# A hybrid attention encoder block on one Trainium2 core: v of the neighbourhood heads kept by head, column and row, and gate products handed out differently

## Chip, core and metric

The kernel runs on one core of one Trainium2 chip. The metric is the device time of one execution in microseconds (us); lower is better. All inputs and weights lie in the chip's memory (DRAM) when it starts, and the output goes back there. The instruction streams are those of TensorE (PE, with its weight loads listed apart as PEld), VectorE (DVE), ScalarE (ACT), GpSimd (POOL), and SyncE (SP), which does nothing but issue transfers.

## What is computed

One encoder layer over 1024 tokens of width 1024, in float32. The parts that matter here:

```python
a = rms_norm(x, g_mix)
qa, ka, va, qd, kd, vd, gate_na, gate_dil = split(a @ w_in)
# mixer A: 8 heads of 64 on a grid of 16 rows x 64 columns; each query sees a
# clamped window of 8 rows x 16 columns, with a learned bias per head
y_na  = neighborhood_attention(heads(qa, 8), heads(ka, 8), heads(va, 8), rpb)
# mixer B: 3 groups of 4 heads, banded attention at dilation 1, 4, 16 (rotary q, k)
y_dil = dilated_attention(rotary(heads(qd, 12)), rotary(heads(kd, 12)), heads(vd, 12))
h = x + (sigmoid(gate_na) * (y_na @ W_A) + sigmoid(gate_dil) * (y_dil @ W_B)) @ w_out
h = h + relu(rms_norm(h) @ w_up) ** 2 @ w_down
h = h + sigmoid(rms_norm(h) @ w_ple_gate) * (p @ w_ple_proj)
out = rms_norm(h)
```

In mixer A a score is q.k/8 plus the bias, and positions outside the window get -1e30 through the bias; then comes a softmax and the product with v.

## The kernel before

Every float32 matrix product is done on rounded operands: an operand is split into a high part (a copy or cast on ACT, line 107 of the helper `split`) and a low part (a subtraction on DVE or POOL, line 108), and three products hi.hi, hi.lo, lo.hi are summed (`mm3`, lines 206 to 208). Buffers come from tile pools of fixed size; a tile that is asked for again waits until the readers of its last use are done. The program is written once, and a scheduler with a model of the engines then decides the order in which each engine gets its instructions; where the code says `keep_in_program_order`, as for all PE work of the attention, that order is the written one. Each engine works through its own list in order, so an instruction that waits holds up all behind it on that engine. SP's list of transfers is such a list too.

The stages, in order of time: the normalised input and the v columns of `w_in` (`v_unit`, five units of 256 columns; u = 0 and 1 are the neighbourhood heads), written to `v_scr` in DRAM as [token][head][128], where the 128 are the high and low halves of 64; then q and k by ten fast-product units (`unit`, their results in `ps_q`), written to `qk_scr`; then attention; then the branch products with `W_A` and `W_B` (`ps_b`), and the rest of the layer, which the change does not touch.

**Attention** is a list of tiles: 96 dilated ones (3 groups of 32) and then 64 neighbourhood ones (8 heads x 4 column blocks `cb` x 2 query halves `qt`). One step of the loop takes three tiles at different stages (`AHEAD` = 3): the tile three steps on gets its scores (PE into `sc`, lines 629 and 630; then DVE adds bias or mask and takes the extreme of the row, line 637; then ACT takes the exponential, line 639), and the present tile is turned (PE transposes into `tp_p`, line 717 for the neighbourhood and 846 to 852 for the dilated groups; ACT and DVE split it into `pt_h` and `pt_l`) and multiplied with v (`av`). In the neighbourhood, DVE takes the reciprocal `rs` of the sum (line 707) and POOL scales the tile by it (line 708) before it is turned. DVE forms the smallest of (score with its sign turned + bias with its sign turned), so that the result can be handed to the exponential as it is. For that, POOL turns the sign of each loaded bias tile in place (line 692).

`na_loads` brings the data of the next column block: a bias tile, and v as four transfers of 64 KB each, one for each group `gq` of four grid rows (line 678).

The **gate products** (`gates()`, into `ps_g`, line 594) depend on nothing in the attention and fill PE there. They come in 256 steps of three products of 512 columns; each 16 steps need one weight unit, loaded into `w_raw` (line 137) and split into `w_hi` and `w_lo` (lines 154, 155). `FILL_HEAD` steps stand ahead of the first tile, `FILL_DIL` are paid for each dilated tile, `FILL_NA` for each neighbourhood tile; what is left comes behind the last tile.

Of the kernel before, what the change touches and what calls it, by code (L numbers as in the profile page):

```python
# [9 lines left out]
F32 = mybir.dt.float32  # L10
F32R = mybir.dt.float32r
I32 = mybir.dt.int32
AF = mybir.ActivationFunctionType
ALU = mybir.AluOpType
# [3 lines left out]
P = 128  # L18
# [6 lines left out]
GW = 64  # L25
NEG = -1e30
EPS = 1e-6

FILL_HEAD = 24
FILL_DIL = 1.5  # L30
FILL_NA = 1.35

AHEAD = 3

# [5 lines left out]
KC0 = (0, 8, 24, 32)  # L40
# [19 lines left out]
def encoder_kernel(ctx: ExitStack, tc: tile.TileContext, t: dict, out: bass.AP):  # L60
    nc = tc.nc
# [23 lines left out]

    p_scr = scr.tile([S, D], F32, name="p_scr")
    v_scr = scr.tile([S, 20 * P], F32, name="v_scr")
    g_scr = scr.tile([16, P, S], F32, name="g_scr")

    qk_scr = scr.tile([20, 2, 2, 64, S], F32, name="qk_scr")  # L90
# [13 lines left out]
    def split(hi, lo, src, scale=None, lo_eng=None):  # L104
        eng = nc.vector if lo_eng is None else lo_eng
        if scale is None:
            nc.scalar.copy(hi, src)  # L107
            eng.tensor_tensor(lo, src, hi.bitcast(F32), op=ALU.subtract)  # L108
        else:
            nc.scalar.activation(hi, src, AF.Copy, scale=scale)  # L110
            eng.scalar_tensor_tensor(lo, src, scale, hi.bitcast(F32), op0=ALU.mult, op1=ALU.subtract)
# [183 lines left out]
    with ExitStack() as st:  # L295
# [83 lines left out]
        def v_unit(u):  # L379
            w2 = take(2, 2)  # L380
            for tp_ in range(4):
                ps = ps_mm.tile([P, HALF], F32, name="ps_v", tag="mm")
                pv3 = ps.rearrange("p (a b) -> p a b", a=2)
                for a in range(2):
                    mm_tok(pv3[:, a, :], w2, tp_ * 2 + a)
                stg = qp.tile([P, 2, 4, P], F32R, name="v_stage", tag="nat")
                s4 = ps.rearrange("p (a h d) -> p a h d", a=2, h=4)
                split(stg[:, :, :, 0:64], stg[:, :, :, 64:128], s4)
                dst = v_scr[tp_ * 256:(tp_ + 1) * 256, u * HALF:(u + 1) * HALF]
                dma(dst.rearrange("(a p) c -> p a c", p=P), stg.rearrange("p a h d -> p a (h d)"))  # L390

# [182 lines left out]
    with ExitStack() as st:  # L574
# [48 lines left out]
        def score(sc, qs, ks, kl, qsl, ksel, n):  # L623
# [5 lines left out]
            pe(nc.tensor.matmul(o, qs[:, qsl], kk, start=True, stop=False))  # L629
            pe(nc.tensor.matmul(o, qs[:, qsl], ll, start=False, stop=True))  # L630

        def soft(sc, bias, n, m_out=None, s_out=None):
            s_ = aa.tile([P, 384], F32, name="s_sb", tag="s_sb", bufs=4)
            nm = m_out if m_out is not None else ap.tile([P, 1], F32, name="nm", tag="nm", bufs=4)
            sm = s_out if s_out is not None else ap.tile([P, 1], F32, name="sm", tag="sm", bufs=4)

            nc.vector.tensor_tensor_reduce(s_[:, :n], sc[:, :n], bias, 1.0, 3.0e38,  # L637
                                           op0=ALU.add, op1=ALU.min, accum_out=nm)
            nc.scalar.activation(s_[:, :n], s_[:, :n], AF.Exp, bias=nm, scale=-1.0, accum_out=sm)  # L639
            return s_, sm  # L640
# [24 lines left out]
        def na_loads(h, cb):  # L665

            if h > 7:
                return
            if cb % 2 == 0:
                na_vt[h, cb // 2] = aa.tile([P, 2, 4, P], F32R, name="v_t", tag="v_t", bufs=3)  # L670
            if cb == 2:
                na_bt[h, 2] = na_bt[h, 1]
            else:
                na_bt[h, cb] = ap.tile([P, 2, 384], F32, name="bias", tag="bias", bufs=3)
                nc.sync.dma_start(na_bt[h, cb], t["na_bias"][h // 2, CT[cb], :, h % 2])
            for gq in range(4):
                src = v_scr.rearrange("(g r c) f -> g c r f", c=GW, r=4)[gq, KC0[cb]:KC0[cb] + 32, :, h * P:(h + 1) * P]
                nc.sync.dma_start(na_vt[h, cb // 2][:, cb % 2, gq, :].bitcast(F32), src)

        def na_score(h, cb, qt, env):  # L680
            j, e = h // 2, h % 2
            if cb == 0 and qt == 0:
                env_head[h] = ready_ops.pop(0)
            if cb == 1 and qt == 0 and h < 7:
                load_raw(h + 1)
            if cb == 2 and qt == 1 and h < 7:
                ready_ops.append(operands(h + 1))
            if qt == 0:
                na_loads(*((h, cb + 1) if cb < 3 else (h + 1, 0)))
                if cb != 2:  # L690
                    bt = na_bt[h, cb]
                    nc.gpsimd.tensor_scalar(bt, bt, -1.0, 1.0, op0=ALU.mult, op1=ALU.mult)
            env["vt"] = na_vt[h, cb // 2]
            qs, ks, kl = env_head[h]
            sc = ps_sc.tile([P, HALF], F32, name="sc", tag="sc")
            o = qt * HALF + cb * P

            def ksel(a):
                return a.rearrange("p (g x) -> p g x", g=4)[:, qt:qt + 3, 4 * KC0[cb]:4 * KC0[cb] + P]

            score(sc, qs, ks, kl, slice(o, o + P), ksel, 384)
            env["pr", cb, qt] = soft(sc, na_bt[h, cb][:, qt, :], 384)

        def na_norm(cb, qt, env):
            pr, sm = env["pr", cb, qt]
# [266 lines left out]
        def pay(upto):  # L972
            while debt[0] >= upto:
                debt[0] -= 1.0
                next(fill, None)

        load_raw(8)
        load_piece(10)
        for b in range(2):
            dma(flat2(act[1][0][b]), a_scr[b])  # L980
        load_raw(9)
# [553 lines left out]
```

## Time and profile before

| what | value |
|---|---|
| time, median of 3 runs | 1693.76 us (1688.40 to 1694.41) |
| the profiled execution: its own time | 1693.16 us |
| the profiled execution: span from first to last instruction | 1691.3 us |
| mean granted TensorE clock | 0.969 of full speed |
| busy: PE, DVE, ACT, POOL | 1566.1, 1191.8, 707.4, 677.9 us |
| moved by transfers | 279.22 MB, 165 GB/s on average |

The busy times are unions over the span: 93% for PE means that PE had a product under way in 93% of the time, not that each ran at full clock. A share of the whole span is a mean over stages with different limits, so the rows further on are cut by stage.

### The profile page before, as it was taken

The numbers are of one execution on the slowest core, as the hardware profiler recorded it, in microseconds if no ns is written. First come the engines' busy times: TensorE is split into PE (matmuls) and PEld (weight loads), VectorE is DVE, ScalarE is ACT, GpSimd is POOL, SyncE is SP. The second block draws the span as 40 slices with busy tenths as digits, with TensorE's granted clock in tenths as the row PEclk, the third lists the DMA queues.
The fourth block names the chain that finished last, engine by engine and source line by source line (L and its number), as shares of the span: only waits on it lengthen the run. The fifth ranks groups of instructions, "written<-read, shape, count | busy, mean of one in ns | idle before, by whom it ended". The sixth has DMA issues, their size and how long they took to land. (4 is left out here: it accounts for less than half of the span.)

```text
span 1691.3 us, 22551 instructions
## 1 busy us (share of the span) xinstructions
PE 1566.1 (93%) x7787; PEld 1308.3 (77%) x7787; DVE 1191.8 (70%) x2016; ACT 707.4 (42%) x1325; POOL 677.9 (40%) x459
## 2 busy tenths in 40 slices
PE   8899999959999988869998799999998999999998
PEld 7899777747788777747787588888876788887886
DVE  6844799622565677755556977667777999999955
ACT  7322222214777766664333433333345333332422
POOL 0332678512333233333402777777743332225100
PEclk9999999988999999989999799999999999999999
DMA  8443455672576678774533244444457545433122
GB/s 310 173 150 108 142 150 161 199 267 89 171 220 186 205 232 253 208 231 156 174 137 131 92 139 147 157 164 143 137 191 279 177 162 163 149 112 118 51 97 71
DMA packets 122353, 279.22 MB, mean 165 GB/s; under 512 B 15392, under 2 KB 39936, under 8 KB 121728
## 3 DMA queue, kind: packets, MB, share of 16 engines
q1 hardware_dynamic: 116480, 267.29, 48.2%
q10 hardware_dynamic: 5760, 10.49, 1.7%
q8 instruction: 62, 1.02, 0.3%
q14 instruction: 51, 0.42, 0.1%
HBM read 186.61 MB, written 91.11 MB: 164 GB/s over the span
## 5 line engine op out<-in xcount | busy, mean ns | idle before, releaser
L107 ACT CAST w_hi<-w_raw 128x512 fp32r<-128x512 f32 (+2 forms) x101 | 81.7, 822 | 135.7 <-POOL w_raw L462 55.5
L108 POOL TENSOR_TENSOR w_lo<-w_raw,w_hi 128x512 fp32r<-128x512 f32 (+2 forms) x32 | 62.4, 1952 | 150.2 <-ACT w_hi L107 93.6
L108 DVE TENSOR_TENSOR f_lo<-f_raw,f_hi 128x512 fp32r<-128x512 f32 x80 | 81.8, 1040 | 50.2 <-ACT f_hi L107 49.6
L108 DVE TENSOR_TENSOR w_lo<-w_raw,w_hi 128x1024 fp32r<-128x1024 f32 (+1 forms) x69 | 82.5, 1202 | 33.3 <-ACT w_hi L107 33.0
L108 DVE TENSOR_TENSOR pt_l<-tp_p,pt_h 128x384 fp32r<-128x384 f32 (+3 forms) x120 | 64.7, 542 | 25.2 <-ACT pt_h L107 24.2
L107 ACT CAST f_hi<-f_raw 128x512 fp32r<-128x512 f32 x80 | 46.2, 613 | 80.9 <-DMA f_raw<-w_up 77.6
L620 POOL TENSOR_TENSOR k_lo<-k_lo,k_st 128x1024 fp32r<-128x1024 f32 x12 | 32.0, 2670 | 99.8 <-ACT k_st L617 81.3
L107 ACT CAST pt_h<-tp_p 128x384 fp32r<-128x384 f32 (+3 forms) x120 | 55.7, 467 | 35.8 <-PE tp_p L717 25.6
L708 POOL TENSOR_SCALAR s_sb<-s_sb,rs 128x384 f32<-128x384 f32 x64 | 41.8, 658 | 71.4 <-DVE rs L707 56.6
L1158 POOL TENSOR_TENSOR u_t<-u_t 128x512 f32<-128x512 f32 x45 | 53.6, 1192 | 38.2 <-ACT u_t L1157 36.9
L1157 ACT ACTIVATE u_t<-u_t 128x512 f32<-128x512 f32 x45 | 28.4, 631 | 74.4 <-DVE u_t L1144 74.0
L1321 DVE TENSOR_TENSOR h<-ps_d,h 128x512 f32<-128x512 f32 x84 | 54.6, 678 | 2.2 <-PE ps_d L208 2.0
L637 DVE CUSTOM_DVE_ANT_0 s_sb<-sc,band 128x256 f32<-128x256 f32 (+1 forms) x64 | 26.4, 413 | 41.7 <-PE sc L630 41.1
L639 ACT ACTIVATE s_sb<-s_sb,stats 128x256 f32<-128x256 f32 (+2 forms) x96 | 44.9, 469 | 23.8 <-DVE stats L637 23.0
L629 PE MATMUL sc<-k_st,q_st 128*128 128x384 f32 (+3 forms) x160 | 52.9, 331 | 0.2 <-DVE stats L637 0.2
L108 DVE TENSOR_TENSOR f_lo<-f_t,f_hi 128x512 fp32r<-128x512 f32 x32 | 51.3, 1607 | 1.8
L206 PE MATMUL ps_b<-y_op,w_hi 128*128 128x512 f32 x96 | 38.8, 413 | 12.2 <-ACT y_op L107 9.9
L639 ACT ACTIVATE s_sb<-s_sb,nm 128x384 f32<-128x384 f32 x64 | 39.4, 616 | 22.7 <-DVE nm L637 21.8
L630 PE MATMUL sc<-k_lo,q_st 128*128 128x384 f32 (+3 forms) x160 | 48.8, 305 | 0.0
L1321 DVE TENSOR_TENSOR sum_t<-ps_d,sum_t 128x512 f32<-128x512 f32 x72 | 46.7, 678 | 2.7 <-PE ps_d L208 2.7
L717 PE MATMUL tp_p<-ident,s_sb 128*128 128x128 f32 x192 | 33.6, 286 | 15.5 <-POOL s_sb L708 12.7
L637 DVE CUSTOM_DVE_ANT_0 s_sb<-sc,bias 128x384 f32<-128x384 f32 x64 | 35.2, 550 | 16.3 <-PE sc L630 14.8
(477 smaller groups left out, 5838.6 us busy)
## 6 DMA issues: line engine op xcount, KB each, us to landing
f_raw<-w_up SPq DMA_DIRECT2D x32, 512.0 KB
w_raw<-w_in SPq DMA_DIRECT2D x26, 512.0 KB
u_raw<-l_scr SPq DMA_DIRECT2D x25, 512.0 KB
qk_scr<-o SPq DMA_DIRECT2D x96, 128.0 KB
h<-l_scr SPq DMA_DIRECT2D x24, 512.0 KB
l_scr<-u_t SPq DMA_DIRECT2D x42, 256.0 KB
l_scr<-u_s SPq DMA_DIRECT2D x42, 256.0 KB
v_scr<-v_stage SPq DMA_DIRECT2D x20, 512.0 KB
```

The source lines that it names most:

```text
L107: nc.scalar.copy(hi, src)
L108: eng.tensor_tensor(lo, src, hi.bitcast(F32), op=ALU.subtract)
L206: nc.tensor.matmul(ps, sh, mh, start=first, stop=False)
L620: (nc.vector if h < 8 else nc.gpsimd).tensor_tensor(kl, kf, ks.bitcast(F32), op=ALU.subtract)
L629: pe(nc.tensor.matmul(o, qs[:, qsl], kk, start=True, stop=False))
L630: pe(nc.tensor.matmul(o, qs[:, qsl], ll, start=False, stop=True))
L637: nc.vector.tensor_tensor_reduce(s_[:, :n], sc[:, :n], bias, 1.0, 3.0e38, op0=ALU.add, op1=ALU.min, accum_out=nm)
L639: nc.scalar.activation(s_[:, :n], s_[:, :n], AF.Exp, bias=nm, scale=-1.0, accum_out=sm)
L708: nc.gpsimd.tensor_scalar(pr, pr, rs, 1.0, op0=ALU.mult, op1=ALU.mult)
L717: pe(nc.tensor.transpose(tp[:, i * P:(i + 1) * P], pr[:, kb * P:(kb + 1) * P], ident))
L1158: nc.gpsimd.tensor_tensor(c, c, c, op=ALU.mult)
L1321: nc.vector.tensor_tensor(d, ps, d, op=ALU.add)
```

## The change

Four things change. (1) v of the eight neighbourhood heads goes to a new buffer `v_na`, laid out as [head][column][row in group][group][128], so that the v of a column block is one transfer with 2 KB in a row for each partition, not four with 512 bytes; the stores of these two units become four for each tile of 256 tokens, in rows of 512 bytes. (2) The bias is used with its own sign: `soft_max` takes bias minus score and the largest of the row, and a small DVE instruction turns the sign of that largest value; POOL's in-place sign change is gone. (3) `prep(11)` splits the first two gate weights ahead of the first loads of the attention. (4) The three numbers that hand out the gate steps are others.

```diff
-FILL_HEAD = 24
-FILL_DIL = 1.5
-FILL_NA = 1.35
+FILL_HEAD = 30
+FILL_DIL = 1.1
+FILL_NA = 1.8
...
+    v_na = scr.tile([8, GW, 4, 4, P], F32, name="v_na")
...
                 split(stg[:, :, :, 0:64], stg[:, :, :, 64:128], s4)
+                if u < 2:
+                    for a in range(2):
+                        for r in range(2):
+                            dma(v_na[4 * u:4 * u + 4, :, 2 * a + r, tp_, :].rearrange("h c f -> c h f"),
+                                stg[r * GW:(r + 1) * GW, a])
+                    continue
...
+        def soft_max(sc, bias, n):
+
+            s_ = aa.tile([P, 384], F32, name="s_sb", tag="s_sb", bufs=4)
+            nm, mx, sm = (ap.tile([P, 1], F32, name=x, tag=x, bufs=4) for x in ("nm", "mx", "sm"))
+            nc.vector.tensor_tensor_reduce(s_[:, :n], bias, sc[:, :n], 1.0, -3.0e38,
+                                           op0=ALU.subtract, op1=ALU.max, accum_out=mx)
+            nc.vector.tensor_scalar(nm, mx, -1.0, None, op0=ALU.mult)
+            nc.scalar.activation(s_[:, :n], s_[:, :n], AF.Exp, bias=nm, scale=1.0, accum_out=sm)
+            return s_, sm
...
-            for gq in range(4):
-                src = v_scr.rearrange("(g r c) f -> g c r f", c=GW, r=4)[gq, KC0[cb]:KC0[cb] + 32, :, h * P:(h + 1) * P]
-                nc.sync.dma_start(na_vt[h, cb // 2][:, cb % 2, gq, :].bitcast(F32), src)
+            nc.sync.dma_start(na_vt[h, cb // 2][:, cb % 2].rearrange("p g f -> p (g f)").bitcast(F32),
+                              v_na[h, KC0[cb]:KC0[cb] + 32].rearrange("c r g f -> (c r) (g f)"))
...
-                if cb != 2:
-                    bt = na_bt[h, cb]
-                    nc.gpsimd.tensor_scalar(bt, bt, -1.0, 1.0, op0=ALU.mult, op1=ALU.mult)
...
-            env["pr", cb, qt] = soft(sc, na_bt[h, cb][:, qt, :], 384)
+            env["pr", cb, qt] = soft_max(sc, na_bt[h, cb][:, qt, :], 384)
...
+        prep(11)
         load_raw(8)
-        load_piece(10)
```

In the built program PE has as many instructions as before, POOL 25 fewer, DVE 65 more, ACT 2 more, and SP 72 fewer. The first place where the order differs is the handover from q and k to attention. On ACT, before, the list there is (`p` belongs to the last q and k unit, `q_st` and `k_st` are the first dilated head's operands, `w_hi` of 128x1024 a gate weight, `g_st` a finished gate half):

```order
L107 CAST w_hi<-w_raw_3157 128x512 x2
L546 COPY p_3361<-ps_q 128x512
L616 ACTIVATE q_st<-q_raw 128x1024
L617 CAST k_st<-k_lo 128x1024
L154 CAST w_hi<-w_raw 128x1024 x2
L596 COPY g_st<-ps_g 128x512
L597 DMA g_scr<-g_st 128x512
```

With the change it is:

```order
L109 CAST w_hi<-w_raw_3182 128x512 x2
L109 CAST w_hi<-w_raw 128x1024 x2
L554 COPY p_3386<-ps_q 128x512
L604 COPY g_st<-ps_g 128x512 x2
L605 DMA g_scr<-g_st 128x512 x2
L156 CAST w_hi<-w_raw 128x1024
L624 ACTIVATE q_st<-q_raw 128x1024
L625 CAST k_st<-k_lo 128x1024
```

The two gate weights moved from behind `q_st` and `k_st` to ahead of `p`; two `g_st` copies and a third weight now stand ahead of `q_st`.

The second place is DVE in the neighbourhood tiles, before (the instruction with `sc,bias` is line 637, the row behind it reads out its result):

```order
L752 TENSOR_TENSOR y_na<-av,fold 64x16x16 x2
L108 TENSOR_TENSOR pt_l<-tp_p,pt_h 128x3x128
L707 RECIPROCAL rs<-sm 128x1
L637 ISA s_sb,nm<-sc,bias 128x384
L637 ISA nm 128x1
L108 TENSOR_TENSOR pt_l<-tp_p,pt_h 128x3x128
L619 SCALAR_TENSOR_TENSOR q_st<-q_raw,q_st 64x1024
L620 TENSOR_TENSOR k_lo<-k_lo,k_st 128x1024
```

With the change, at a like place (two tiles, each with its new instruction `nm<-mx`):

```order
L721 RECIPROCAL rs<-sm 128x1
L644 ISA s_sb,mx<-bias,sc 128x384
L644 ISA mx 128x1
L110 TENSOR_TENSOR pt_l<-tp_p,pt_h 128x3x128 x2
L646 TENSOR_SCALAR nm<-mx 128x1
L644 ISA s_sb,mx<-bias,sc 128x384
L644 ISA mx 128x1
L627 SCALAR_TENSOR_TENSOR q_st<-q_raw,q_st 64x1024
L646 TENSOR_SCALAR nm<-mx 128x1
L628 TENSOR_TENSOR k_lo<-k_lo,k_st 128x1024
```

The sign change often stands behind another instruction: of the 64, 15 follow their read-out at once, 12 stand behind a `rs`, 25 behind one or two `pt_l` (with at most an `rs` or another tile's `nm` beside them), and 12 behind something else, mostly longer (`q_st`, `w_lo`, rows of the merge).

The third place is ACT at the end of attention, where the sigmoid of the first gate tiles (`gt`) is drawn into the last tiles and needs another function table than the exponential. Before:

```order
L1038 ACT_TABLE_LOAD
L1038 ACTIVATE gt<-gt 128x1024
L107 CAST pt_h<-tp_p 128x3x128
L107 CAST w_hi<-w_raw 128x768
L107 CAST pt_h<-tp_p 128x3x128
L639 ACT_TABLE_LOAD
```

With the change:

```order
L1052 ACT_TABLE_LOAD
L1052 ACTIVATE gt<-gt 128x1024
L762 COPY fold<-av 64x512
L647 ACT_TABLE_LOAD
L647 ACTIVATE s_sb,sm<-s_sb,nm 128x384
L109 CAST pt_h<-tp_p 128x3x128
L109 CAST w_hi<-w_raw 128x768
L109 CAST pt_h<-tp_p 128x3x128
L1052 ACT_TABLE_LOAD
```

In all, three table loads stood there before and five stand there now, so one more sigmoid goes in among exponentials.

## Rows read from the trace of the kernel before

**Rows 1.** The page's first part: PE's busy time, share, instructions.

```profile
PE 1566.1 (93%) x7787; PEld 1308.3 (77%) x7787; DVE 1191.8 (70%) x2016; ACT 707.4 (42%) x1325; POOL 677.9 (40%) x459
```

**Rows 2.** Windows by stage: length, busy PE, PEld, DVE, ACT, POOL, clock, DMA share, GB/s.

```profile
0.00:163.00 163.00, 150.19 (x1120) 143.27 (x1120) 97.39 (x200) 66.34 (x124) 38.34 (x28) 0.98 0.52 184
...
361.50:399.50 38.00, 19.17 (x73) 15.22 (x73) 1.91 (x2) 6.11 (x7) 9.47 (x4) 0.73 0.57 194
...
399.50:571.50 172.00, 166.68 (x976) 139.50 (x976) 98.17 (x287) 128.55 (x322) 47.94 (x20) 0.98 0.58 178
...
571.50:748.00 176.50, 147.58 (x862) 124.68 (x861) 129.41 (x335) 112.69 (x251) 65.03 (x88) 0.95 0.74 227
```

**Rows 3.** Timeline of PE at the handover: start, length, instruction, [idle before <- releaser].

```profile
361.12 0.39 PE L208 MATMUL ps_q<-act01h,w_lo 128*128 128x512 f32 x1
...
377.66 0.80 PE L594 MATMUL ps_g<-act00h,w_hi 128*128 128x512 f32 x1 [16.16 <-ACT w_hi L154]
...
381.56 0.80 PE L594 MATMUL ps_g<-act00h,w_lo 128*128 128x512 f32 x1 [2.67 <-POOL w_lo L155]
...
394.11 0.39 PE L594 MATMUL ps_g<-act00h,w_hi 128*128 128x512 f32 x1
...
399.55 0.25 PE L629 MATMUL sc<-k_st,q_st 128*128 128x192 f32 x1
```

**Rows 4.** Timelines of ACT, POOL and SP at the handover.

```profile
374.67 1.06 ACT L616 ACTIVATE q_st<-q_raw 128x1024 fp32r<-128x1024 f32 x1 [17.98 <-DMA q_raw<-qk_scr]
...
376.57 1.99 ACT L154 CAST w_hi<-w_raw 128x1024 fp32r<-128x1024 f32 x2
...
376.74 2.46 POOL L620 TENSOR_TENSOR k_lo<-k_lo,k_st 128x1024 fp32r<-128x1024 f32 x1 [27.69 <-ACT k_st L617]
...
350.88 0.33 SPq L289 DMA_DIRECT2D act10l<-a_scr  x1
...
369.33 8.00 SPq L605 DMA_DIRECT2D q_raw<-qk_scr  x4
```

**Rows 5.** Windows of the second third of the dilated tiles, columns as above.

```profile
467.50:522.80 55.30, 54.76 (x332) 46.62 (x331) 33.88 (x93) 43.91 (x104) 18.03 (x7) 1.00 0.62 193
```

**Rows 6.** Waits of the neighbourhood stage: who for whom, total us, times, longest.

```profile
POOL bias L692 <- DMA bias<-na_bias: 24.3, 11, 4.3
...
PE tp_p L717 <- POOL s_sb L708: 12.7, 8, 3.8
...
PE av L740 <- DVE pt_l L108: 8.6, 7, 3.9
```

**Rows 7.** Timelines of POOL and PE around 670 us.

```profile
669.56 1.20 POOL L692 TENSOR_SCALAR bias<-bias 128x768 f32<-128x768 f32 x1 [1.26 <-DMA bias<-na_bias]
...
670.74 1.70 POOL L708 TENSOR_SCALAR s_sb<-s_sb,rs 128x384 f32<-128x384 f32 x3
...
671.37 0.90 PE L717 MATMUL tp_p<-ident,s_sb 128*128 128x128 f32 x3 [3.84 <-POOL s_sb L708]
```

**Rows 8.** One line's instructions, and a DVE group of the neighbourhood stage (busy, mean ns).

```profile
L242 DVE TENSOR_SCALAR nv<-nv x32: 136/144/147, 10.7 to 1685.4; 128x1 f32<-128x1 f32 x32
...
L108 DVE TENSOR_TENSOR pt_l<-tp_p,pt_h 128x384 fp32r<-128x384 f32 x64 | 34.8, 549 | 11.5 <-ACT pt_h L107 11.4
```

**Rows 9.** Timeline of ACT at the first sigmoid.

```profile
727.92 1.28 ACT L1038 ACT_TABLE_LOAD   x1
...
729.22 1.06 ACT L1038 ACTIVATE gt<-gt 128x1024 f32<-128x1024 f32 x1
```

**Rows 10.** Transfers' issue on SP: ns min/median/max, first and last start.

```profile
L678 SPq DMA_DIRECT2D v_t<-v_scr x128: 512/601/1608, 551.0 to 722.8; - x128
...
L289 SPq DMA_DIRECT2D v_scr<-v_stage x20: 359/360/387, 48.6 to 163.3; - x20
```

**Rows 11.** Timeline of PE: last gap of the v stage, and the end of attention.

```profile
35.51 0.39 PE L207 MATMUL ps_v<-w_lo,act00h 128*128 128x256 f32 x1 [0.32 <-DVE w_lo L108]
...
756.96 0.80 PE L206 MATMUL ps_b<-y_op,w_hi 128*128 128x512 f32 x1 [9.04 <-ACT y_op L107]
```

## The prediction

> **What bounds the kernel now.** The page comes first: PE is busy for 1566.1 us of 1691.3, the others are far from it [rows 1]. The change adds no product and takes none away, so it can only win time that PE stands idle or runs at its lower clock, or lose more of it. Next come the windows by stage [rows 2]. The reader is to see that PE is not equally full. In the v stage it is busy for 150.2 of 163 us, and after 35.51 us the timeline shows it no gap [rows 11]. In the 38 us of the handover it works for 19.2, at 0.73 of its clock. In the 172 us of the dilated tiles it works for 166.7 with ACT at 128.6, three quarters. In the 176.5 us of the neighbourhood tiles it works for 147.6 at 0.95 of its clock: 28.9 us idle, and by the clock 0.05 x 176.5 = 8.8 us of full-speed work lost. Third, what ended the gaps: the timeline at the handover [rows 3, 4] and the waits of the neighbourhood stage [rows 6].
>
> **The handover.** The last q and k product starts at 361.12 and the next would follow 0.23 us later, but PE waits 16.16 us for the first gate weight, then 2.67 us for its low half [rows 3]. That weight was not late from memory. ACT sat 17.98 us on `q_st`, whose data, issued at 369.33, came at 374.67, and the two casts stood behind it [rows 4]. With the change both casts stand ahead. The buffers that they fill are released by the last unit's t2, t3 and b22, t1, all before its end, so the first is in time for 361.4. The 30 steps then end 30 x 0.68 = 20.4 us later, at 381.8; a step is (399.55 - 394.11) / 8 = 0.68 us [rows 3]. The second condition for a score is the first head's low part: POOL ended it at 376.74 + 2.46 = 379.2 [rows 4]. Its loads, the stores ahead of them and `q_raw`'s release stay where they were, SP gets two weight loads in front of them (0.36 us each by the like issues [rows 10]), and ACT now does `q_st` behind a third cast of about 1 us that waits for the last unit's end. I take 380 to 382, so PE's own 381.8 decides: the first score comes at 381.8 and not at 399.55, **-17.7 us**. `act10l`, needed from step 9 on at 366.8, is issued at 350.88 [rows 4] and gets one weight load in front of it; I cost that at nothing, and if it is late the gap is PE's. Bounds: 0 (something else holds the first product) and -18.
>
> **The dilated tiles.** 96 tiles lose 0.4 step each: 38.4 steps x 0.68 = 26.1 us of PE. PE was full here (5.3 of 172 us idle), so all of it counts if nobody else takes over. ACT loses with them 2.4 weight casts at 1.0 us [rows 4] and about 4.8 `g_st` copies, half as wide and so by estimate 0.5 us each, some 5 us of its 128.6, and keeps 123.3. The highest share that ACT reached in a third of the stage is 43.9 of 55.3, 79% [rows 5]; held there, the stage takes 155.3 us, -16.7. At PE's own pace it takes 146 us, with ACT at 85%. An engine that works in order for three tiles at once does not do that without waits; I take the middle, **-21 us** (151 us, ACT at 82%). Bounds: -26, and -7 if ACT stays at its present 75%.
>
> **The neighbourhood tiles.** They get 64 x 0.45 = 28.8 more steps, 19.6 us of PE. Against that stand these:
>
> - POOL's sign change goes. POOL waited 24.3 us in 11 places for the bias to land, with the scaling of a tile queued behind it, and PE's turns waited 12.7 us for that scaling [rows 6]. Around 670 us the whole of it is seen: bias at 669.56, scaling at 670.74, PE starts at 671.37 after 3.84 us [rows 7]. I take back the 12.7, and 2.5 us of the 8.8 lost at the lower clock.
> - The rest of the idle time, 28.9 - 12.7 = 16.2 us, has several causes, the largest being PE's wait for `pt_l` (8.6 us [rows 6]). More filling between the tiles gives DVE and ACT more time for each: I take half, 8 us.
> - DVE gets 64 sign changes of one column. The nearest rows, the same instruction elsewhere, last 144 ns [rows 8], so 9.2 us on an engine that is busy for 129.4 of 176.5. What counts is that the exponential waits for it. A tile is scored three tiles ahead, so most of that is slack; I take a third, +3 us. Bounds: 0, and the case below.
> - One more sigmoid among the exponentials means two more table loads on ACT, 1.28 us each, with the next instruction at 729.22, right at the end of the load [rows 9]. That is 2.6 us late in the stage; half, +1.3 us.
>
> The Trainium skill, in "ScalarE: Activation LUTs", section "What ACT_TABLE_LOAD costs", has a table switch at about 2.66 us, the load and a drain of about the same length; this trace shows the load of that length and no drain behind it in ACT's list. By the page's figure the two switches would cost 5.3 us of ACT, and half of that 2.7 us in place of 1.3, an estimate.
>
> The sum for this stage is 19.6 - 12.7 - 2.5 - 8 + 3 + 1.3 = **+0.7 us**. Bounds: -18 (all idle time and all clock loss regained), +31 (none, and 9.2 + 2.6 on the path).
>
> **At nothing.** v's loads in one piece take 96 issues of about 0.6 us off SP [rows 10]; no row shows PE waiting for a v tile, so I count no gain, though it lets the bias be issued earlier. The stores of the first two v units become 32 in place of 8, 24 x 0.36 = 8.6 us more of SP in the v stage [rows 10]. They hold up weight loads that stand behind them, but PE had no gap there and the transfer engines were half free (0.52) [rows 2]; if that cover is gone, up to 8.6 us. Six steps are left behind the last tile where two were: 2.7 us more, inside the 9.04 us in which PE waits for `y_op` [rows 11].
>
> **Sum.** -17.7 - 21 + 0.7 = -38.0 us. The profiled execution took 1693.16 us, which stands 0.6 us beside the median of the runs, so both serve: 1693.2 - 38.0 = **1655 us**.
>
> **The rivals.**
>
> - *ACT keeps the dilated tiles slow.* Its waits for DVE's statistics grow as the tiles come faster, its share stays at 75%, and the stage takes 165 us: -7 in place of -21, 1669 us. For it: at 79% it is already the second fullest engine [rows 5]. Against it: PE had hardly a gap there, so the waits of the others show nothing of their limits. 0.18.
> - *The neighbourhood stage closes up.* Filling at 1.8 steps a tile covers nearly all waits, and the lower clock goes with them: -10 in place of +0.7, 1644 us. For it: 37.7 us are there to be had. Against it: the longest gaps come from DVE, which gets more work. 0.14.
> - *The handover does not move.* If the first product waits for a released buffer, a load or the restored `act10`, the 17.7 us are gone: 1673 us. Against it: the row names ACT, and ACT waited for another tile. 0.08.
> - *The sign change comes onto the path; slower.* Where it stands behind a `pt_l`, which itself waits for ACT's cast, the exponential of a tile waits for an earlier tile's turn: 0.144 + 0.549 [rows 8] + 0.37 for the cast (by width from the 1.0 us of 1024 columns [rows 4], an estimate) = 1.06 us a tile. If the three tiles of lead are used up, that is 64 x 1.06 = 68 us, 1655 - 3 + 68 = 1720 us. It decides at 41 / 64 = 0.64 us a tile for no gain, and at 0.78 for half a per cent slower. For it: of the 64, 37 stand behind a `pt_l` or something longer. Against it: a neighbourhood tile takes 176.5 / 64 = 2.8 us, so the lead is some 8 us. 0.08.
>
> **How the numbers follow.** The forecast itself has 0.52, with 1646 to 1664 as its own range. From 1640 to 1677 lie the forecast, the ACT case, the handover case and most of the better one; left out are the slower case and the far end of the better, together under 2 in 10. A measurement of this kernel can tell about half a per cent, 8.5 us, from no change. Every case but the last is faster than that by itself; a mix of the handover and ACT cases comes to -6, and a part of the sign-change case ends between. So faster 0.88, same 0.06, slower 0.06.
>
> **What would show it.** Right: PE goes from `ps_q` to `ps_g` with under 1 us between; the first score comes near 382; ACT does both weight casts before `p`; the dilated stage takes about 151 us with ACT at 80% or more; the neighbourhood stage takes 170 to 183 us, with no PE wait for POOL's scaling over 2 us, and DVE's `nm` at about 0.14 us. Wrong: a PE gap at 361 that ends with a DMA or a store; exponentials that wait for `nm` in most tiles; a dilated stage over 160 us; a bias transfer that DVE waits for; PE gaps in the v stage that end with `w_hi`, whose load stood behind the new stores.

## The result, and the profile after

The changed kernel takes 1673.5 us (median of 4 runs, 1672.6 to 1674.1), the one before 1694.1 beside it: a ratio of 0.9884, 95% interval 0.986 to 0.9908, or 20.6 us off. A second series of the changed kernel gave 1671.9 us and 0.9882 [0.9861, 0.9903]. Forecast were 1655 us and 38 us off; the way and the range hold, the size is half.

The profiled execution took 1673.03 us, its span is 1670.8 us, 20.5 less than before. The page's first part shows PE's busy time hardly moved [rows 1]: the products are the same.

```profile
PE 1571.5 (94%) x7787; PEld 1312.3 (79%) x7787; DVE 1200.9 (72%) x2081; ACT 708.4 (42%) x1327; POOL 654.0 (39%) x434
```

The windows by stage, cut at the same events as [rows 2] (the first score, the first neighbourhood score, the last gate product; then the rest of the span):

```profile
361.50:381.90 20.40, 20.40 (x91) 16.89 (x90) 1.91 (x2) 6.00 (x7) 4.67 (x2) 1.00 0.99 342
381.90:538.90 157.00, 145.47 (x860) 120.91 (x858) 94.17 (x284) 120.07 (x313) 47.76 (x19) 0.96 0.57 186
538.90:725.10 186.20, 168.75 (x961) 143.12 (x959) 136.76 (x402) 119.32 (x260) 44.88 (x66) 0.96 0.71 227
725.10:1670.80 945.70, 893.95 (x3921) 730.08 (x3920) 712.80 (x1027) 348.19 (x543) 391.21 (x237) 0.97 0.43 144
```

The reader is to see four differences to [rows 2]. The handover is full: PE busy for all of 20.4 us at full clock, 17.6 less than before. The dilated stage is 15.0 us shorter. The neighbourhood stage is 9.7 us longer. The rest, whose order did not change, is 2.4 us longer (943.3 before). In the sum -17.6 - 15.0 + 9.7 + 2.4 = -20.5 us. The last cut lies ahead of the wait for `y_op`, which fell from 9.04 to 6.5 us, since 5.2 left-over steps fill more of it than 1.6; behind the first branch product 934.3 us became 939.1.

**The handover.** PE's timeline, at its begin and its end:

```profile
361.28 0.39 PE L210 MATMUL ps_q<-act01h,w_lo 128*128 128x512 f32 x1
361.51 0.39 PE L602 MATMUL ps_g<-act00h,w_hi 128*128 128x512 f32 x1
...
381.68 0.39 PE L602 MATMUL ps_g<-act11h,w_lo 128*128 128x512 f32 x1
...
381.91 0.25 PE L637 MATMUL sc<-k_st,q_st 128*128 128x192 f32 x1
382.18 0.19 PEld L638 LDWEIGHTS sc<-k_lo,q_st 128*128 128x128 f32 x1 [0.31 <-POOL k_lo L628]
```

ACT has cast the gate weights by then, ahead of the copy `p`:

```profile
353.77 1.05 ACT L109 CAST w_hi<-w_raw 128x1024 fp32r<-128x1024 f32 x1 [4.84 <-PE ps_q L209]
356.26 0.59 ACT L554 COPY p<-ps_q 128x512 f32<-128x512 f32 x1 [1.44 <-PE ps_q L210]
```

From `ps_q` to `ps_g` there is no gap where 16.16 us were [rows 3]. 30 steps later, at 381.91, comes the first score; POOL's `k_lo` is ready only 0.3 us after it, so both conditions end together.

**The dilated stage.** PE is idle for 11.5 us (157.0 - 145.5), before for 5.3. The longest gap, on ACT's and PE's timelines:

```profile
388.30 1.04 ACT L625 CAST k_st<-k_lo 128x1024 fp32r<-128x1024 f32 x1
389.24 0.51 ACT L657 ACTIVATE s_sb<-s_sb,stats 128x256 f32<-128x256 f32 x1
389.74 1.03 ACT L156 CAST w_hi<-w_raw 128x1024 fp32r<-128x1024 f32 x1
390.67 0.58 ACT L109 CAST pt_h<-tp_p 128x512 fp32r<-128x512 f32 x1
391.31 0.39 PE L900 MATMUL av<-pt_h,v_t 128*128 128x256 f32 x1 [2.25 <-ACT pt_h L109]
...
393.94 0.63 PE L602 MATMUL ps_g<-act00h,w_lo 128*128 128x512 f32 x1
```

The cast `pt_h` for which PE waits stands behind `k_st` and `w_hi`. Behind the gap a gate product takes 0.63 us and not 0.39. The windows of six us around show the granted clock of that stretch: 0.72, full again in the next.

```profile
391.00:397.00 6.00, 5.35 (x21) 4.26 (x22) 2.37 (x5) 2.37 (x7) 3.21 (x2) 0.72 0.60 218
397.00:403.00 6.00, 6.00 (x38) 5.17 (x37) 2.99 (x13) 4.33 (x13) 0.00 (x0) 1.00 0.02 5
```

The same happens at 422.6 to 429.4, behind gaps of 1.69 and 1.49 us, and at 536 to 540 (clock 0.58), where the gaps are two of 0.7 us.

**The neighbourhood stage.** The waits there:

```profile
POOL s_sb L722 <- DVE rs L721: 88.9, 41, 6.3
ACT s_sb L647 <- DVE nm L646: 31.0, 26, 3.1
POOL s_sb L722 <- DVE nm L646: 30.2, 13, 8.2
...
PE tp_p L731 <- POOL s_sb L722: 8.7, 5, 4.1
...
PE av L754 <- DVE pt_l L110: 4.1, 6, 1.7
...
PE av L753 <- ACT pt_h L109: 2.7, 3, 1.2
```

POOL's wait for the bias (24.3 us [rows 6]) is gone, but PE still waits 8.7 us for POOL's scaling where it waited 12.7. POOL now waits for DVE's `rs` and for the exponential, which waits for `nm`. The longest case, around 658 us:

```profile
653.39 0.61 ACT L647 ACTIVATE s_sb<-s_sb,nm 128x384 f32<-128x384 f32 x1
...
655.34 1.22 DVE L627 SCALAR_TENSOR_TENSOR q_st<-q_raw,q_st 64x1024 fp32r<-64x1024 f32 x1
656.59 1.23 DVE L628 TENSOR_TENSOR k_lo<-k_lo,k_st 128x1024 fp32r<-128x1024 f32 x1
657.73 0.16 DVE L721 RECIPROCAL rs<-sm 128x1 f32<-128x1 f32 x1
657.81 0.14 DVE L646 TENSOR_SCALAR nm<-mx 128x1 f32<-128x1 f32 x1
...
658.04 0.62 ACT L647 ACTIVATE s_sb<-s_sb,nm 128x384 f32<-128x384 f32 x1 [3.05 <-DVE nm L646]
658.06 1.47 POOL L722 TENSOR_SCALAR s_sb<-s_sb,rs 128x384 f32<-128x384 f32 x1 [8.22 <-DVE nm L646]
```

The exponential of one tile ended at 654.0 (its sum was read out at 654.1), and its sum could be inverted then. DVE did that at 657.73, behind the next head's `q_st` and `k_lo`. The next tile's `nm`, 0.14 us long, stands behind the same two, and its exponential comes 3.05 us late. PE's turn at 659.58 had waited 4.06 us by then. What PE waits for here is DVE's list at a change of heads, not the sign of the bias. In three of the four waits of this kind over 0.5 us, 6.1 of the 8.7 us, `rs` stands behind the next head's `k_lo`; in the fourth it stands behind rows of the merge and another tile's score.

### The profile page after: what moved, and what is told of

Read it like the earlier page. It is cut to its first block, busy times and chain, and to the rows that moved or that the text cites. A ratio compares the mean times of both kernels' runs of the same rounds, so it can differ in the third digit from the quotient of the medians.

```text
span 1670.8 us, 22589 instructions
## 1 busy us (share of the span) xinstructions
PE 1571.5 (94%) x7787; PEld 1312.3 (79%) x7787; DVE 1200.9 (72%) x2081; ACT 708.4 (42%) x1327; POOL 654.0 (39%) x434
## 5 line engine op out<-in xcount | busy, mean ns | idle before, releaser
L109 ACT CAST pt_h<-tp_p 128x384 fp32r<-128x384 f32 (+3 forms) x120 | 56.1, 467 | 24.3 <-PE tp_p L731 14.5
L210 PE MATMUL ps_d<-w_hi,m_op 128*128 128x512 f32 x112 | 43.6, 399 | 2.7 <-DVE m_op L110 2.7
L496 POOL TENSOR_TENSOR o<-x,c 128x512 f32<-128x512 f32 x24 | 40.6, 1707 | 11.2 <-DVE c L491 8.7
L1297 POOL TENSOR_TENSOR t_raw<-pair,w_raw 128x1024 f32<-128x1024 f32 x6 | 15.6, 2598 | 75.0 <-DVE act11l L110 30.8
```

The lines of the kernel that those rows point to most:

```text
L210: nc.tensor.matmul(ps, sl, mh, start=False, stop=last)
L496: nc.gpsimd.tensor_tensor(dst, x, y, op=op)
```

## The experiments

All times are medians beside the kernel before on the same chip, which took 1694.0 to 1695.7 us there. "Changed" is the changed kernel, and its edits are shown against it; the first four are edits of the kernel before. The lengths of the stages in the profiled executions, in us, worked out from the first and last rows of PE's timeline (the last q and k product starts at 361.0 to 363.7 us, at 365.9 with the gate casts on POOL; it is no part of a row):

| kernel | time | ratio to before | last q,k to first score | dilated | neighbourhood | to first branch product | rest |
|---|---|---|---|---|---|---|---|
| before | 1694.1 | | 38.4 | 171.6 | 176.4 | 9.4 | 934.3 |
| changed | 1673.5 | 0.9884 [0.986, 0.9908] | 20.6 | 157.0 | 185.9 | 6.9 | 939.1 |
| changed, again | 1671.9 | 0.9882 [0.9861, 0.9903] | 20.6 | 156.6 | 185.7 | 8.2 | 937.2 |
| weights first, alone | 1681.2 | 0.9926 [0.9911, 0.9941] | 20.0 | 173.0 | 177.7 | 10.5 | 938.6 |
| sign, alone | 1694.8 | 0.9998 [0.9984, 1.0012] | 38.9 | 166.9 | 175.4 | 9.7 | 937.9 |
| filling, alone | 1690.2 | 0.997 [0.9954, 0.9986] | 43.0 | 158.4 | 185.6 | 6.4 | 933.7 |
| v, alone | 1698.8 | 1.002 [1.0003, 1.0038] | 37.8 | 171.5 | 184.9 | 9.0 | 935.8 |
| sign on ACT | 1667.9 | 0.9847 [0.9823, 0.9871] | 20.6 | 154.8 | 186.8 | 6.9 | 934.1 |
| gate casts on POOL | 1665.7 | 0.9826 [0.9804, 0.9848] | 21.6 | 157.0 | 182.6 | 5.2 | 933.4 |
| old v | 1673.4 | 0.9872 [0.9847, 0.9897] | 20.6 | 155.9 | 188.3 | 6.9 | 937.1 |
| filling 0.9 / 2.1 | 1658.3 | 0.9781 [0.9757, 0.9805] | 20.6 | 144.3 | 186.8 | 7.3 | 934.9 |
| the same, late casts on POOL | 1663.5 | 0.9827 [0.9805, 0.985] | 20.6 | 147.2 | 189.2 | 7.9 | 936.5 |
| 0.8 / 2.25, late casts on POOL | 1670.2 | 0.9871 [0.9849, 0.9892] | 20.6 | 138.2 | 203.2 | 8.2 | 933.0 |
| 0.9 / 2.1, late casts on POOL, sign on ACT | 1660.4 | 0.9815 [0.979, 0.984] | 20.6 | 142.7 | 189.1 | 6.8 | 933.7 |

The expectations cut the two attention stages elsewhere: the dilated one runs from the first score to the first turn (`tp_p`) of a neighbourhood tile, the neighbourhood one from there to the last such turn. By that cut the changed kernel has 160.9 and 174.6 us (174.7 in the expectations), the kernel before 175.6 and 169.0. Where an expectation names a length, it is compared by that cut.

**Weights first, alone.**

```diff
+        prep(11)
         load_raw(8)
-        load_piece(10)
```

> The kernel before with one part of the change alone: the first two gate weights are split ahead of the attention's first loads; filling numbers, sign and v as before. Theory A (the parts pay in separate places, and the handover is most of the gain): 24 steps end at 361.5 + 24 x 0.68 = 377.8, then PE waits some 4 us for the first head's low part (ended 382.1 in the changed kernel), the first score comes near 382, and all behind it is as before: about 17 us off, 1676 to 1679 us. Rival B (the handover's gain is only there with the other filling numbers, since the dilated tiles then wait for their operands): the first score comes near 382, but the dilated stage grows, and under 10 us are left: 1685 us or more.

Measured: 0.74% off, 14.5 us by the medians; the first score comes at 382.13. PE's waits in the stage behind it:

```profile
PE sc L629 <- DVE q_st L619: 3.3, 1, 3.3
PE sc L630 <- POOL k_lo L620: 1.8, 1, 1.8
```

With 24 steps the products end before the first head's operands are there, 5.1 us in all. The dilated stage, which holds the second of these waits, is 1.4 us longer than before. The time lies 2 us over A's bound and 4 under B's; the mechanism of B, a dilated stage that grows, isn't there, and what A misses lies behind the first neighbourhood score (1.3 us in that stage, 4.3 behind attention). The six more steps of the changed kernel (4.1 us) lie just in this gap.

**Sign, alone.** The helper `soft_max` with its DVE instruction, and no sign change on POOL, as in the change's diff.

> The kernel before with the sign part alone: bias with its own sign, largest value, small sign change on DVE, none on POOL. Theory A: POOL's wait for the bias goes and PE's wait for the scaled tile shrinks from 12.7 us; DVE's 64 instructions take back a part: 3 to 9 us off, 1685 to 1691 us. Rival C (the small instruction takes the place of the wait removed: exponential, sum, scaling are as late as before): within 3 us of before, or slower.

Measured: no difference. PE's wait for the scaling is nearly as long as before, with another cause:

```profile
POOL s_sb L715 <- DVE rs L714: 81.4, 35, 7.4
POOL s_sb L715 <- DVE nm L638: 40.3, 19, 6.5
...
PE tp_p L724 <- POOL s_sb L715: 11.6, 9, 2.7
```

Between the read-out of the extreme and the start of the exponential lie 96.5 us, summed over the 64 tiles; before 35.3, in the changed kernel 71.8. The time is as rival C has it, and exponential and scaling are late again. But the trace doesn't put this down to the small instruction. Six of PE's waits for the scaling, 10.1 of the 11.6 us, stand at a change of heads, where DVE takes the next head's `q_st` and `k_lo` ahead of the `rs` that the scaling needs. One of them:

```profile
615.92 1.22 DVE L619 SCALAR_TENSOR_TENSOR q_st<-q_raw,q_st 64x1024 fp32r<-64x1024 f32 x1
617.17 1.23 DVE L620 TENSOR_TENSOR k_lo<-k_lo,k_st 128x1024 fp32r<-128x1024 f32 x1
618.32 0.16 DVE L714 RECIPROCAL rs<-sm 128x1 f32<-128x1 f32 x1
618.64 0.59 POOL L715 TENSOR_SCALAR s_sb<-s_sb,rs 128x384 f32<-128x384 f32 x1 [5.12 <-DVE rs L714]
619.28 0.55 PE L724 MATMUL tp_p<-ident,s_sb 128*128 128x128 f32 x3 [1.81 <-POOL s_sb L715]
```

In the kernel before, DVE takes the same tile's `rs` ahead of `q_st`, and PE does not wait there:

```profile
621.14 0.14 DVE L707 RECIPROCAL rs<-sm 128x1 f32<-128x1 f32 x1
...
621.76 1.34 DVE L619 SCALAR_TENSOR_TENSOR q_st<-q_raw,q_st 64x1024 fp32r<-64x1024 f32 x1
```

Three of the six tiles wait like this before too, 5.0 us in all. So half of the new wait came with another order of DVE's list. No run puts `rs` ahead of `q_st` and `k_lo`, so what that would give isn't shown. That the dilated stage is 4.7 us shorter in this execution (its granted clock is 1.00, 0.98 before) and the rest 3.6 longer has no part of the edit behind it that I could name.

**Filling, alone.** The three numbers of the change.

> The kernel before with the three filling numbers alone. Theory A: six more steps ahead of the first score, +4; the dilated tiles lose 26 us of products and give 11 back as waits, -15; the neighbourhood tiles get 19.6 us and hide about half behind the waits that are still there, +6 to +10: in all within 5 us of before. Rival D (moving the steps is where the gain behind the handover comes from): 8 us off or more.

Measured: 0.3% off, 5.1 us. The handover gets 4.6 us longer, the dilated stage 13.2 us shorter, the neighbourhood 9.2 us longer: the stages as theory A had them, the sum at the edge of its bound, and rival D falls. POOL still turns the bias here:

```profile
POOL bias L692 <- DMA bias<-na_bias: 36.4, 18, 4.7
...
PE tp_p L717 <- POOL s_sb L708: 5.5, 4, 2.4
```

POOL waits more for the bias than before, and PE less for POOL: more filling covers that wait. The profiled execution is only 1.4 us shorter than the one before; the gain of 5.1 us is that of the medians. The stage takes 185.6 us with POOL's sign change and 185.9 without it in the changed kernel.

**v, alone.** The buffer `v_na`, its stores and its loads.

> The kernel before with v of the neighbourhood heads kept by head, column and row, alone. Theory A: no PE wait ends on a v tile, so within 3 us of before. Rival E (SP's list, shorter by 72 transfers, brings the bias earlier, and with it POOL's sign change): PE's wait for the scaled tile falls from 12.7 us to under 6 and 5 to 10 us come off. Rival F: the 32 stores in short rows delay weights in the v stage, and the first q product comes 1 us or more later than 163.1.

Measured: 0.2% longer, 3.4 us by the ratio, at the edge of what can be told and just over theory A's bound; its reason holds, no wait of PE in the attention ends on a v tile. Rival E falls: SP's list is shorter, but POOL waits longer for the bias.

```profile
POOL bias L698 <- DMA bias<-na_bias: 43.1, 16, 5.9
```

PE's wait for the scaling is 17.4 us, and the neighbourhood stage is 8.5 us longer in this execution, which took 1703.44 us, 4.6 over the median. In SP's list the two single v transfers of a block now stand ahead of two biases, and wait there 24.8 us in all for `av` or a turn to release their buffer (12.1 before, where biases stood between the four pieces). The bias transfers themselves wait 27.6 us for DVE's `nm` or `rs` (6.7 before). Which of the two makes the bias late isn't shown. Rival F falls too: the first q product comes at 163.7, 0.6 us later.

**Sign on ACT.**

```diff
-            nc.vector.tensor_scalar(nm, mx, -1.0, None, op0=ALU.mult)
+            nc.scalar.activation(nm, mx, AF.Copy, scale=-1.0)
```

> The changed kernel with the small sign change done by ACT, ahead of the exponential, and not by DVE. Theory G (the sign change took the place of the bias wait: over the 64 tiles the exponentials now start 71.8 us after their read-outs in sum, 35.3 before, since DVE's instruction comes 0.39 us behind the read-out in the median and lasts 0.14): the sum falls to 40 to 55 us, PE's wait for the scaled tile falls from 8.7 us to 5 or less, the neighbourhood stage from 174.7 to 170 to 173. Rival H (a tile is scored three tiles ahead, and that lateness is slack; what counts is ACT's own list, which gets some 64 x 0.2 us more): within 2 us of the changed kernel in that stage, or longer.

Measured: the sum of lateness is 77.3 us, not under 55; PE's wait for the scaling is 10.2 us; the neighbourhood stage is not shorter (186.8; 177.0 by the expectation's cut). Theory G falls, and the stage is as H has it. But the lateness did not shrink, so this run can't show that it is slack. What it shows is that nothing is won by turning the sign on the other engine: in four of the six waits for the scaling `rs` again stands behind the next head's `q_st` or `k_lo`. For slack speaks the run with the filling alone, whose exponentials are late by 27.6 us in sum (71.8 in the changed kernel) and whose stage is as long, though with POOL's sign change in it. The time is 4 to 6 us under the changed kernel's, but its profile has that in the dilated stage (2.2 us) and behind attention (5.0, less 2.4 lost ahead of it), and the intervals of the two ratios overlap, so no gain is claimed.

**Gate casts on POOL.**

```diff
-                tc.keep_in_program_order(nc.scalar.copy(wh[:, :cols], raw[:, :cols]))
+                nc.gpsimd.tensor_copy(wh[:, :cols], raw[:, :cols])
```

> The changed kernel with the casts of the gate weights during attention on POOL (30% busy there) and not on ACT. Theory J (the dilated tiles give back 11 us because ACT comes late where q_st, k_st and w_hi stand in a row: PE waits at 391.3 and 422.6 for pt_h, 2.25 and 1.69 us, and runs at half clock for some 2.5 us behind each): the stage falls from 160.9 to 156 to 158.5 us, and PE's waits for pt_h there from 5.2 to under 3. Rival K (ACT's share is not it; the lists of three engines in turn are): within 1.5 us of 160.9, with the waits moved to other releasers; POOL's k_lo may come late and add to it.

Measured: PE's waits for `pt_h` in the dilated stage fall from 5.2 to 1.6 us, as theory J had it, but the stage is as long as before the edit (157.0; 162.0 against 160.9 by the expectation's cut):

```profile
PE av L903 <- DVE pt_l L110: 4.6, 7, 2.2
PE sc L638 <- POOL k_lo L628: 1.8, 1, 1.8
PE av L900 <- ACT pt_h L109: 1.6, 3, 0.7
```

Other waits came in, DVE's `pt_l` and POOL's `k_lo`. Rival K holds. The time is 6 to 8 us under the changed kernel's, and the intervals of the ratios lie apart; in the profile 3.3 us of that are the neighbourhood stage, 1.7 the wait behind it, and 5.7 the rest, with 1.0 lost in the handover and 4.6 ahead of it, so that only 4 us are to be placed in stages that the edit touches.

**Old v.** The change without its first part: `v_scr` as before, four transfers for a block.

> The changed kernel with v of the neighbourhood heads loaded from the old buffer, by four transfers for each column block, and stored as before. Theory L (v's single transfers make the bias late for POOL when POOL turns its sign, 43.1 us of waits against 24.3, which cost 3 us alone; with the sign used as it is nobody waits for the bias, so there is nothing left to lose or win): within 3 us of the changed kernel. Rival M (the new layout costs by itself, by the stores or the transfers): 3 to 6 us faster than the changed kernel. Rival N (it helps here): 3 us or more slower.

Measured: as the changed kernel. Theory L holds. The neighbourhood stage is 2.4 us longer and the dilated one 1.1 shorter in this execution. The two profiles of the changed kernel differ by 0.2 and 0.4 us there, so whether that belongs to the edit stays open; the time doesn't tell.

**Filling moved on.**

```diff
-FILL_DIL = 1.1
-FILL_NA = 1.8
+FILL_DIL = 0.9
+FILL_NA = 2.1
```

> The changed kernel with the filling moved on in the same direction: 0.9 steps for a dilated tile and 2.1 for a neighbourhood tile. 19 steps, 13.1 us of products, leave the dilated tiles. Theory O (what leaves the dilated tiles counts about half, since PE then waits there; what comes to the neighbourhood counts about a quarter while there is idle time, more later): dilated 160.9 to 153 to 156, neighbourhood 174.7 to 178 to 184, in sum within 3 us of the changed kernel. Rival P (the numbers of the change stop short of the best): 4 us or more faster. Rival Q (they are past it): 4 us or more slower.

Measured: rival P, and by far: 15 us under the changed kernel, and the intervals of the two ratios lie apart. By its median it is the best version of this study; by its profile 11.4 us come from the attention's stages and the wait behind them, and the untouched stretch behind gives 4.2, with 1.6 lost ahead. By the expectation's cut the stages are 148.8 and 175.4 us. The windows of the dilated and the neighbourhood stage:

```profile
383.50:527.70 144.20, 130.80 (x805) 110.09 (x804) 91.60 (x283) 118.74 (x311) 43.91 (x18) 0.98 0.59 191
527.70:714.90 187.20, 175.83 (x1014) 149.43 (x1012) 137.40 (x402) 119.85 (x263) 47.59 (x68) 0.99 0.74 237
```

13.1 us of products left the dilated stage, and it is 12.7 us shorter; as many came to the neighbourhood, and it is 0.9 us longer. PE's idle time in the dilated stage grew by 1.9 us, where the first move had added 6.2. Theory O's rates of a half and a quarter were read from the first move and did not hold for the second. ACT is busy for 82% of the dilated stage (118.74 of 144.2), so the 76% of the changed kernel were no limit. In the neighbourhood PE's clock went from 0.96 to 0.99 and its idle time from 17.5 to 11.4 us: 6.1 us less idle, and 0.03 x 187 = 5.6 us of clock, pay for nearly all of the 13.1.

**The changed kernel again.**

> The changed kernel unaltered, once more. Open is why 4.8 us were given back behind the attention, where all lists are the same (first branch product to first down product: 498.7 us before, 503.4 changed; 499.0 to 503.4 in the other runs, without a pattern by part). Theory R (that stretch varies from one execution to the next by some 4 us, by where a wait lets the clock fall): a stretch anywhere from 499 to 504, and the time within 3 us of 1673.5. Rival S (the change makes it longer): again 502.5 or more.

Measured: from the first branch product to the first down product 501.1 us, where the first profile had 503.4, and the time is 1.6 us under 1673.5. Rival S falls by its own bound, and theory R's hold; what makes that stretch vary isn't shown.

**The same filling, late gate casts on POOL.**

```diff
+                if 18 <= n <= 25:
+                    nc.gpsimd.tensor_copy(wh[:, :cols], raw[:, :cols])
+                else:
+                    tc.keep_in_program_order(nc.scalar.copy(wh[:, :cols], raw[:, :cols]))
```

> Filling at 0.9 and 2.1, and POOL casts the gate weights of the neighbourhood stage (from the ninth unit on) in place of ACT. From the run with the filling moved on (1658.3 us) and the one with the casts on POOL (neighbourhood 174.7 to 168.0, dilated not shorter): neighbourhood 175.4 to 169 to 172, dilated as with the filling moved on, 148.8; 1653 to 1656 us. Rival (the two use up the same idle time of PE, 9.6 us of which are left): 1657 us or more.

Measured: 1663.5 us, the rival, by an interval that touches that of the filling alone. Both stages are longer than with the filling alone, 2.9 and 2.4 us (the neighbourhood 176.7 by the expectation's cut): POOL's casts pay nothing at this filling.

**Filling 0.8 and 2.25, late casts on POOL.**

> As the run before, with filling at 0.8 and 2.25. 6.5 us of products leave the dilated tiles, as many come to the neighbourhood, where PE would be idle for some 6 us then. If ACT, busy for 82% of the dilated stage at 0.9, is near its limit, that stage shrinks by under 3 us and the neighbourhood grows by 3 to 6: slower than the run before by 1 to 4 us. If not: 3 us or more faster.

Measured: 6.7 us more than the run before, past the best, and as neither side of the expectation had it: the dilated stage did shrink, and the neighbourhood took more than that back. The dilated stage still gives 9.0 us for 6.5 us of products. The neighbourhood takes 14 us more. Its window:

```profile
522.20:725.60 203.40, 186.53 (x1045) 158.60 (x1044) 139.31 (x402) 117.75 (x262) 55.55 (x73) 0.97 0.67 216
```

The clock is 0.97 where the run before had 1.00, some 6 us, and PE's longest group of waits there is for DVE's `pt_l`, 9.0 us (4.6 in the run before).

**All three.** The first of these two, with the sign change on ACT.

> As the first of these two, with the sign change on ACT as well. With the lateness of the exponential being slack, as the run with ACT's sign change showed it in the neighbourhood stage (177.0 against 174.7): within 2 us of it. If PE's time there is short of slack now that it has more filling: 3 us or more apart, faster if DVE was the one that came late, slower if ACT.

Measured: 1660.4 us, 3 us under the run before, with overlapping intervals, and not better than the filling alone. It tells nothing apart.

## Why the prediction was right in its way and half in size

Four terms made -38.0 us; the profile has -20.5. The parts alone come to 12.5 + 0.3 + 5.1 - 3.4 = 14.5 us off by their ratios. Each of the four is uncertain by 2.4 to 3.0 us. What is missing to some 20 is for the most part the handover, where the profiles of the parts come to 13.9 us and the change to 17.8: the filling alone pays 4.6 us for its six more steps there, and the weights alone leave a gap of 5.1 us that these steps would fill.

- **The handover: right.** -17.7 forecast, -17.6 measured, by the mechanism named: ACT's casts ahead of `p`. That PE's own 30 steps decide was nearly a tie (0.3 us).
- **The dilated tiles: right mechanism, mis-sized.** -21 forecast, -15.0 measured. The step that failed is the one that set the pace by ACT's share, with 79 to 85% as its range. ACT is at 76% (120.07 of 157.0) and PE still waits. ACT's own work was off as well: it fell by 8.5 us and not by 5, 1.3 of which are a table load that moved ahead of the first score. Of the 26.1 us, 11.1 were given back: PE's idle time grew by 6.2 us, its busy time fell by 21.2 and not 26.1, and some 3 us of that difference are clock (0.98 to 0.96). The gaps stand at a few places, the longest where `q_st`, `k_st` and `w_hi` come in a row, and cost twice, in idle time and in the clock behind them. The rival with 1669 us came near the measured total, but by luck: its dilated stage of 165 us is 8 us too long, and its reason doesn't hold, since ACT's share of 76% is no limit: 0.9 steps took it to 82%. Nor are the two places with ACT the whole cause, since without them the stage was as long, with DVE and POOL late in their stead. All executions with 1.1 steps and ACT's casts have 11.3 to 11.6 us of idle time there, and their lengths, 154.8 to 158.4 us, go with the clock, 0.98 to 0.95. What fixes that idle time stays open.
- **The neighbourhood tiles: mis-sized.** +0.7 forecast, +7.3 measured, with the 2.4 us that come back in the wait for `y_op` (which was the cover named for the left-over steps). The term that failed is the 12.7 us taken back for POOL's sign change. PE's wait for the scaling fell by 4.0 us, and the sign part alone took 1.1; the filling alone, with POOL's sign change still there, took 7.2. The waits that the prediction read did go: in six of the eight, 9.2 of the 12.7 us, the sign change stood right ahead of the scaling, and in five of these `rs` had been ready for 1.6 to 4.6 us. So it was with the 3.84 us at 671.37 [rows 7], whose `rs` is this:

```profile
665.96 0.16 DVE L707 RECIPROCAL rs<-sm 128x1 f32<-128x1 f32 x1
```

  What the prediction had at nothing is that others would come in elsewhere: those behind `q_st` and `k_lo` in DVE's list. The half taken of the other idle time was about right (waits for `pt_l` and `pt_h` from 13.1 to 6.8 us), though the 8.6 us named there for `pt_h` are a wait for `pt_l` [rows 6]. The clock gave 0.96 for 0.95.
- **The sign change as a rival, slower: fell.** `nm` takes 0.147 us in the median, and exponentials do wait for it, 31.0 us in 26 places, but few of those waits reach PE, and with ACT turning the sign the stage was no shorter. What it did to PE's waits apart from the new order of DVE's list isn't shown.
- **Table loads: as forecast in length.** Five loads stand at the end of attention where three stood; two of them:

```profile
693.60 1.28 ACT L1052 ACT_TABLE_LOAD   x1 [2.16 <-issue]
694.89 1.06 ACT L1052 ACTIVATE gt<-gt 128x1024 f32<-128x1024 f32 x1
695.97 1.28 ACT L647 ACT_TABLE_LOAD   x1
```

  The next instruction starts 0.01 us behind a load. The Trainium skill, "ScalarE: Activation LUTs", section "What ACT_TABLE_LOAD costs", adds a drain of about the load's length to it. The load's 1.28 us agree with the page, and the drain does not show: ahead of the first load stand 2.16 us that the profile puts down to issue, ahead of the other four 0.02.
- **v, its stores and loads: at nothing, and right.** With POOL's sign change in place they cost about 3 us, without it nothing that the time shows. That SP's shorter list would bring the bias earlier was wrong in its direction. The cover named for the stores was misread: behind 35.51 us PE does stand idle in the v stage [rows 11], though for an operand of DVE and not for a weight:

```profile
57.61 1.12 PE L273 MATMUL tp<-ident,xn 128*128 128x128 f32 x4 [5.21 <-DVE act10l L108]
```

  With the new stores that gap is 5.32 us, and the first q product comes at 163.4 and not at 163.1, so nothing came of it.
- **Not forecast: 4.8 us behind the first branch product.** Its lists are the same in both. The second execution has 2.9 us of it, and over all runs that stretch to the end lies between 933.0 and 939.1 us, for parts of the change and for edits alike. The stretch ahead of the last q and k product, where only the stores of v and the first gate weights differ, varies by 4.9 us. So it differs from one execution to the next; that none of it belongs to the change isn't shown.

## What to carry to other kernels

A wait that is named in the profile is worth at most the time until the next condition is met: before a whole wait is taken back, look at what else its instruction needs, how late that is, and whether the change gives an engine's list another order. Here the second move of filling products paid nearly in full, where they closed gaps in which PE would idle and then run on at its lower clock; the first had paid about half. So the amount for each stage is best found by a few runs along one line, past the first gain (1.5, 1.1, 0.9 and, with the late casts on POOL, 0.8 steps here), and not from the share of another engine. Parts of a change can share a cover: six more steps cost 4.6 us where nothing had been made free, and nothing where the operands were late anyway.

## What was not expected of the hardware

Behind some gaps PE's products stayed slow for a while. After the gaps of 2.25 us at 391.3, of 1.69 and 1.49 us at 422.6 and 424.5, of 2.42 us at 594.3 and of 4.06 us at 659.6, 512-column products took 0.63 us, where they take 0.39 otherwise, for some 3 to 7 us. The granted clock is 0.72 over the six microseconds behind the first of them, so PE spent part of that at the lower of its two levels, 1.2 GHz. These gaps cost more than their length. Not every gap did: behind 1.36 us at 553.7 and 1.73 us at 684.3 the products took 0.39 us, and behind two gaps of 0.7 us at 536 they were slow. Which gaps cost it isn't settled here. A [128,1] instruction on DVE that needs the read-out right ahead of it started 0.03 us behind its end in the 15 places where it followed at once; in the others it came later by what the list had put between.
